# Two halves of a product added by ScalarE and VectorE, not by a matrix product, in the small expert blocks of a mixture-of-experts layer

## The chip, the cores and the metric

The kernel runs on one core of a Trainium2 chip. The metric is the device time of one launch in microseconds (us); the time given for a kernel is the median of its runs. Beside the plain runs, one execution was profiled: the profile shows for each engine when it worked and what it waited for. The engines are TensorE (PE, with its weight loads as PEld), VectorE (DVE), ScalarE (ACT), GpSimd (POOL), and SyncE (SP), which here only issues transfers.

## The reference

One layer of a diffusion backbone over 1024 tokens of width 1024, in fp32: a modulated RMSNorm, one input projection, two kinds of mixing (differential attention and retention), an output projection with a gated residual, and then a mixture of experts. Only the last part matters here. Each token picks 8 of 64 experts; every expert is a small gated network of inner width 256, and a shared one is applied to all tokens:

```python
xb = h_pad[tok]
yb = (jax.nn.silu(xb @ w1[e]) * (xb @ w3[e])) @ w2[e]
acc.at[tok].add(yb * wt[:, None])
```

The result is added to the residual and normalised once more.

## The kernel before, in words

**Precision.** PE multiplies in a reduced fp32 format. So each operand is split in two: hi is the operand as ACT copies it into that format, lo is what DVE finds as the difference. A product of x and w is then hi x hi + hi x lo + lo x hi. The weights of an expert (3 MB, loaded as `eraw`) are split in six pieces of 128x1024 each, ACT's copy on L1110 and DVE's subtraction on L1111; both write tiles named `w`. While the blocks of one expert run, the pieces of the next are split between them.

**Blocks.** The experts are ranked by their number of tokens and each rank has a fixed capacity, 384 down to 32 rows, cut in blocks of 128 rows and a rest. A list puts large and small experts in turn. After the shared expert's 8 blocks come 96 blocks of routed rows; 33 of these have a rest of 64 or 32 rows and run as `n == 64`.

**A step of the loop** (L1181 and around) does for block i: the up product (`up()`: 8 slices of the width, w1 and w3 side by side in a PSUM bank of 128x512), the gate (`gate()`: SiLU on ACT, L1207, product on DVE, L1209, into `hn`), the transposes of `hn` on PE (L1165) with their split on ACT and DVE (L1169, L1170, `ehT`), and, one step later, the down product (`down()`: two banks `py` of 128x512). DVE scales each bank by the routing weight and the layer's gate into `y` (L1232), and POOL adds the rows of `y` to the token table `acc` in DRAM (the scatter, L1120). The rows of the block after next are gathered on POOL (L1149, `xg`) and transposed on PE (`tr`, L1165, then `xT`). A scatter starts when all scatters of the expert before have landed. There are two `y` buffers, used in turn, so a block's `y` can be written when the scatter of the block two before it has landed.

**Blocks of 64.** Here hi and lo of x stand side by side as 128 columns of one operand. Two products per slice of the width, with the hi and lo of w, then give x_hi w in rows 0 to 63 of the bank and x_lo w in rows 64 to 127, and the two halves of rows have to be added. Before, ACT copies rows 64 to 127 of the bank into a buffer `fb` (L1185), and PE multiplies it with a matrix `fold` (L1190) that moves row 64 + r onto row r and adds it in the bank. This is done once for `up` and twice for `down`, 99 times in all. The zeros in the rest of `fb` and of `fold` keep the other rows as they are; in the gate all 128 rows are worked on.

**Order.** The order of the instructions on each engine is set by a scheduler that simulates them when the program is built; it is fixed then, and each engine works through its own list in turn. So an instruction that waits also holds up what stands behind it on its engine.

Of the kernel before, what the change touches and what calls it, by code (L numbers as in the profile page):

```python
# [9 lines left out]
F32 = mybir.dt.float32  # L10
F32R = mybir.dt.float32r
# [3 lines left out]
AF = mybir.ActivationFunctionType  # L15
OP = mybir.AluOpType
# [4 lines left out]
P = 128  # L21
# [63 lines left out]
def hybrid_layer_kernel(ctx: ExitStack, tc: tile.TileContext, A, out, dbg=None):  # L85
    nc = tc.nc
    pe, dve, act, pool, sp = nc.tensor, nc.vector, nc.scalar, nc.gpsimd, nc.sync
# [19 lines left out]
    def open_pool(ctx, name, side=None, space=None):  # L107

        kw = {k: v for k, v in (("side", side), ("space", space)) if v is not None}
        return ctx.enter_context(tc.tile_pool(name=name, bufs=1, reuse_waits="tile", **kw))  # L110
# [17 lines left out]
    consts = ctx.enter_context(tc.tile_pool(name="consts", bufs=1, side="left"))  # L128
# [4 lines left out]
    def C(k):  # L133
        o, n = CST_OFF[k]
        return cst[:, o:o + n]

    ident = C("ident")
# [70 lines left out]
    def project(t, w, n0=0, n1=512):  # L208
        his, los = w
        hh, hl = hT(t)  # L210
        ps = psa.tile([P, 512], F32, name="pp", tag="pp", bufs=2)
        for k in range(KT):
            wh, wl = his[k // 2][:, k % 2, n0:n1], los[k // 2][:, k % 2, n0:n1]
            pe.matmul(ps[:, n0:n1], hh[:, k, :], wh, start=(k == 0), stop=False)  # L214
            pe.matmul(ps[:, n0:n1], hh[:, k, :], wl, start=False, stop=False)  # L215
            pe.matmul(ps[:, n0:n1], hl[:, k, :], wh, start=False, stop=(k == KT - 1))  # L216
        return ps
# [50 lines left out]
    for kind in range(2):  # L268
        for fb in range(2):
            dve.tensor_scalar(Wd[:, kind, :, fb], lg[:, 4 * fb:4 * fb + 4], pw[:, 2 * kind + fb:2 * kind + fb + 1],  # L270
                              None, op0=OP.mult)
# [158 lines left out]
    for i, g in enumerate(pairs):  # L430
        for t in (2 * g - 2, 2 * g - 1):
            if t < 0:
                ps = project(t, W, 256, 512)
# [31 lines left out]
    for i in range(0, TAB_ROWS // P, 126):  # L465
        n = min(126, TAB_ROWS // P - i)
# [21 lines left out]
    for t in range(-2, NT):  # L488
        ada_rest(VADA)
        ps = project(t, W)  # L490
# [13 lines left out]
        for h in range(H):  # L504
            pe.matmul(pk[:, h, :], kd[:, h].rearrange("p a b -> p (a b)"), v[:, h * P:(h + 1) * P],
                      start=True, stop=True)
# [24 lines left out]
    for t in reversed(range(NT)):  # L531
# [4 lines left out]
        ps = project(t, W)  # L536
# [69 lines left out]
    for t in range(-2, NT):  # L606
        ps = project(t, W)
# [6 lines left out]
        c = slice((t + 2) * P, (t + 3) * P)  # L614
# [16 lines left out]
    def row_tile(pl, i, name, **kw):  # L631
        t = pl.tile([P, D], F32, name=name, **kw)
        sp.dma_start(t, bass.AP(tensor=rows_d.tensor, offset=rows_d.offset + i * D, ap=[[0, P], [1, D]]))
        return t
# [167 lines left out]
    def bank(ring, shape):  # L802
        n = ring_at[ring] = ring_at.get(ring, -1) + 1
        b = RINGS[ring][n % len(RINGS[ring])]
        return (psd if b < 6 else ps8).tile(shape, F32, name=ring, tag=f"bank{b}")
# [51 lines left out]
    pm = open_pool(m_ctx, "pm", "right")  # L857
    pl_ = open_pool(m_ctx, "pl", "right")
    pc = open_pool(c_ctx, "pc", "right")
    y2 = Ring(pm, "y0", "y1")  # L860
    g2r = row_tile(pm, 3, "g2r")
# [189 lines left out]

    tokc = consts.tile([P, NT], I32, name="tokc")
    dve.tensor_copy(tokc, C("tok"))

    fold = consts.tile([P, P], F32R, name="fold")
    dve.tensor_scalar(fold, ident, 0.0, None, op0=OP.mult)
    dve.tensor_copy(fold[64:128, 0:64], ident[64:128, 64:128])

    hT4 = Ring(pm, "g0", "g1", "g2", "g3")

    fbs, fb_n = [], [0]

    def fold_buffer():
        if not fbs:
            for tag in ("so", "mks"):
                fbs.append(pl_.tile([P, 512], F32R, name="fb", tag=tag))
                dve.tensor_scalar(fbs[-1][0:64], g2r[0:64, 0:512], 0.0, None, op0=OP.mult)
        fb_n[0] += 1
        return fbs[fb_n[0] % 2]

# [46 lines left out]
    def scatter_add(y, idx, j=None):  # L1117


        x = pool.indirect_dma_start(out=acc, out_offset=bass.IndirectOffsetOnAxis(ap=idx, axis=0), in_=y,  # L1120
                                    in_offset=None, compute_op=OP.add)
        if j is None:
            return
        mine = added.setdefault(j, [])
        for o in mine:
            tc.declare_no_dep(x.ins, o.ins, reason="the blocks of an expert have no row in common")
        for o in added[j - 1] if j else x1_stores:
            tc.add_manual_dep(x.ins, o.ins.name, mybir.DependencyInfo(
                mybir.DependencyClass.Sync, mybir.DependencyReason.DATA), reason="rows of the expert before")
        mine.append(x)  # L1130

    class Block:
# [40 lines left out]
        def product(self, ps, ops, whi, wlo, nk):  # L1173
            if self.n > 64:
                seq = [(o, w) for o, w in ((0, whi), (0, wlo), (1, whi))]
            else:
                seq = [(0, whi), (0, wlo)]
            po = ps[:ops[0].shape[2]]
            for k in range(nk):
                for j, (o, w) in enumerate(seq):  # L1180
                    pe.matmul(po, ops[o][:, k, :], w(k), start=(k == 0 and j == 0),  # L1181
                              stop=(k == nk - 1 and j == len(seq) - 1))
            if self.n == 64:
                fb = fold_buffer()
                act.activation(fb[64:128], ps[64:128], AF.Copy)  # L1185
                self.fb = fb

        def fold(self, ps):
            if self.n == 64:
                pe.matmul(ps, fold, self.fb, start=False, stop=True, skip_group_check=True)  # L1190

        def tr(self):
            if self.xT is None:
# [7 lines left out]

        def gate(self):
            pu = self.pu
            self.fold(pu)
            sl = pm.tile([P, 256], F32, name="sl", tag="sl", bufs=2)
            m = P if self.n == 64 else self.n
            act.activation(sl[:m], pu[:m, 0:256], AF.Silu)  # L1207
            self.hn = pm.tile([P, 2, P], F32, name="hn", tag="hn", bufs=2)
            dve.tensor_tensor(self.hn[:m].rearrange("p k q -> p q k"),  # L1209
                              pu[:m, 256:512].rearrange("p (q k) -> p q k", k=2),  # L1210
                              sl[:m].rearrange("p (q k) -> p q k", k=2), op=OP.mult)
# [4 lines left out]
        def down(self):  # L1216
            n = self.n
            hi2, lo2 = self.W[2:]
            y = y2.tile([P, D], F32, name="y")
            ps, fbs = [], []  # L1220
            for i in range(2):
                c = slice(i * 512, (i + 1) * 512)
                py = bank("py", [P, 512])
                self.product(py, self.hT, lambda k: hi2[k][:, c], lambda k: lo2[k][:, c], 2)
                ps.append(py)
                fbs.append(getattr(self, "fb", None))
            for i in range(2):
                self.fb = fbs[i]
                self.fold(ps[i])
                c = slice(i * 512, (i + 1) * 512)  # L1230
                if YMODE[i]:
                    dve.scalar_tensor_tensor(y[:n, c], ps[i][:n], self.wt, g2r[:n, c], op0=OP.mult, op1=OP.mult)  # L1232
                else:
                    act.activation(y[:n, c], ps[i][:n], AF.Copy, scale=self.wt)
                    pool.tensor_tensor(y[:n, c], y[:n, c], g2r[:n, c], op=OP.mult)
            scatter_add(y[:self.rows], self.idx[:self.rows], self.j)
# [198 lines left out]
    with tc.For_i(0, n_over, 1) as j:  # L1435
# [15 lines left out]
        for q in range(2):  # L1451
            pt = bank("tr", [P, 4, P])
            for i in range(4):
                k = 4 * q + i
                pe.transpose(pt[:, i, :], xg[:, k * P:(k + 1) * P], ident)
            act.activation(xT[:, 4 * q:4 * q + 4, :], pt, AF.Copy)
        pu = bank("up", [P, 512])
        for i in range(2):
            for k in range(KT):
                pe.matmul(pu[:, i * 256:(i + 1) * 256], xT[:, k, :], w13[:, i, k, :], start=(k == 0),  # L1460
                          stop=(k == KT - 1))
        s_ = pf.tile([P, 256], F32, name="fs")
        act.activation(s_, pu[:, 0:256], AF.Silu)
        hn = pf.tile([P, 2, P], F32, name="fhn")
# [7 lines left out]
        y = pf.tile([P, D], F32, name="fy")  # L1472
        for n in range(2):
            c = slice(n * 512, (n + 1) * 512)
# [52 lines left out]
```

## Time and profile before

| | us |
|---|---|
| median of 3 runs (lowest to highest) | 1809.39 (1807.29 to 1812.17) |
| the profiled execution | 1804.75 |
| its span, from first to last instruction | 1802.9 |
| routed experts, in the profile | from about 914 to 1775 |
| PE, DVE, ACT busy over the span | 1667.1, 1349.9, 960.8 |

The busy share of PE is that of pipelined products: one takes some 0.4 us from start to end, and the next starts while it runs. Where a row gives several numbers behind a window they are the busy time of each engine in it; a window without the shares is read against its own length. The chain of waits is followed back from the last instruction, at each step to what released it.

### The profile page before, as it was taken

Reading aid. Unit: us, or ns where it says so; the run is one execution under the profiler, and the core shown is the slowest. Engines: PE = TensorE matmul, PEld = TensorE weight load, DVE = VectorE, ACT = ScalarE, POOL = GpSimd, SP = SyncE. Lnnn points to the kernel's source line nnn. Section 1 sums busy time; section 2 is a strip of 40 time slices with the busy share of each in tenths; the row PEclk is TensorE's granted clock in tenths of the full one; section 3 lists DMA queues with packets and bytes.
Section 4 is the critical chain, followed back from the end, with each engine's and each line's share of the span. In section 5 each row is a group of like instructions: output and inputs, shape, how many; then the busy total and the mean of one; then the engine's idle time right before and its main releaser. Section 6 shows DMA issues by size and latency. Waiting matters only on the chain.

```text
span 1802.9 us, 23066 instructions
## 1 busy us (share of the span) xinstructions
PE 1667.1 (92%) x8022; PEld 1267.4 (70%) x8022; DVE 1349.9 (75%) x2080; ACT 960.8 (53%) x1537; POOL 535.6 (30%) x384
## 2 busy tenths in 40 slices
PE   5899889999799989999899999999999999999992
PEld 3687667788466658777677767777777777777771
DVE  7876666650887866987478888888888988878873
ACT  6532233321688752233266686677675666566652
POOL 0100113300221230457235334333445343332331
PEclk9999999999899999999899999999999999999996
DMA  9665545800111144334889999999999999999976
GB/s 311 211 213 179 182 148 116 181 24 27 69 53 59 36 166 163 105 122 115 268 234 310 317 327 329 319 316 295 342 318 329 356 330 326 329 303 320 315 213 213
DMA packets 128413, 400.57 MB, mean 222 GB/s; under 512 B 13110, under 2 KB 49654, under 8 KB 103336
## 3 DMA queue, kind: packets, MB, share of 16 engines
q1 hardware_dynamic: 81000, 297.10, 46.0%
q0 software_dynamic: 46144, 97.80, 23.2%
q10 hardware_dynamic: 1152, 4.19, 0.6%
q8 instruction: 64, 1.05, 0.2%
q14 instruction: 53, 0.43, 0.1%
HBM read 324.45 MB, written 74.60 MB: 221 GB/s over the span
## 4 chain that ended last, share of the span: by engine, by line
PE 54%; DMA 16%; DVE 14%; ACT 7%; issue 5%; POOL 3%; SPq 1%; POOLq 0%; DVEq 0%; ACTq 0%
PE up L1181 18%; DMA acc<-y,sidx 9%; PE py L1181 8%; PE pp L215 4%; PE pp L214 3%; PE pp L216 3%; PE tr L1165 3%; DVE w L1111 3%; PE pS L97 3%; PE py L97 3%; DMA eraw<-in_exp_w_dram 2%; PE pu L97 2%; ACT w L1110 2%; DVE nmx L697 2%; PE ptt L97 1%
## 5 line engine op out<-in xcount | busy, mean ns | idle before, releaser
L1181 PE MATMUL up<-w,xT 128*128 128x512 f32 (+1 forms) x2136 | 531.1, 398 | 7.7 <-DVE xT L1170 7.3
L1111 DVE TENSOR_TENSOR w<-eraw,w 128x1024 fp32r<-128x1024 f32 x390 | 459.7, 1216 | 42.8 <-ACT w L1110 42.2
L1110 ACT ACTIVATE w<-eraw 128x1024 fp32r<-128x1024 f32 x390 | 400.1, 1056 | 118.4 <-PE up L1181 60.6
L1181 PEld LDWEIGHTS up<-w,xT 128*128 128x128 f32 (+1 forms) x2136 | 381.4, 183 | 106.3 <-DVE xT L1170 12.9
L1120 POOL DMA_INDIRECT acc<-y,sidx x96 | 205.3, 2138 | 484.0 <-DMA acc<-y,sidx 198.7
L1181 PE MATMUL py<-w,ehT 128*128 128x512 f32 (+1 forms) x1116 | 296.0, 408 | 0.8 <-DVE ehT L1170 0.8
L1181 PEld LDWEIGHTS py<-w,ehT 128*128 128x128 f32 (+1 forms) x1116 | 200.4, 187 | 48.5 <-DVE ehT L1170 1.1
L1232 DVE SCALAR_TENSOR_TENSOR y<-py,swt,g2r 128x512 f32<-128x512 f32 (+2 forms) x192 | 137.6, 739 | 62.6 <-DMA acc<-y,sidx 46.6
L214 PE MATMUL pp<-whi,hTh 128*128 128x512 f32 (+1 forms) x448 | 178.9, 400 | 1.3 <-ACT hTh L371 1.2
L216 PE MATMUL pp<-whi,hTl 128*128 128x512 f32 (+1 forms) x448 | 177.0, 397 | 1.2 <-DVE hTl L372 1.2
L215 PE MATMUL pp<-wlo,hTh 128*128 128x512 f32 (+1 forms) x448 | 177.8, 398 | 0.0
L697 DVE TENSOR_REDUCE nmx<-pS 128x1 f32<-128x1280 f32 x64 | 95.1, 1486 | 74.6 <-PE pS L97 74.4
L1149 POOL DMA_INDIRECT xg<-h2tab,sidx x96 | 128.4, 1338 | 72.6 <-PE tr L1165 48.1
L1170 DVE TENSOR_TENSOR xT<-tr,xT 128x512 fp32r<-128x512 f32 (+1 forms) x167 | 104.2, 654 | 17.7 <-ACT xT L1169 17.4
L1207 ACT ACTIVATE sl<-up 128x256 f32<-128x256 f32 (+1 forms) x104 | 39.7, 382 | 139.6 <-PE up L1181 138.8
L159 POOL TENSOR_TENSOR rs_r<-rs_v,mhalf 128x1 f32<-128x1 f32 (+1 forms) x34 | 28.2, 830 | 276.0 <-DVE rs_v L157 160.5
L969 POOL DMA_INDIRECT slots<-dat,ad x64 | 72.0, 1126 | 97.4 <-DVE dat L966 55.2
L216 PEld LDWEIGHTS pp<-whi,hTl 128*128 128x128 f32 x448 | 84.3, 188 | 23.6 <-issue 2.6
L214 PEld LDWEIGHTS pp<-whi,hTh 128*128 128x128 f32 x448 | 84.4, 189 | 22.8 <-issue 2.6
L97 PE MATMUL pS<-K,qsl 128*128 128x512 f32 x336 | 93.1, 413 | 7.3 <-ACT an L704 4.8
L1165 PEld LDWEIGHTS tr<-cst,xg 128*128 128x128 f32 (+2 forms) x800 | 79.7, 140 | 28.2 <-issue 7.1
L215 PEld LDWEIGHTS pp<-wlo,hTh 128*128 128x128 f32 x448 | 84.9, 190 | 19.5 <-issue 2.0
(308 smaller groups left out, 2327.6 us busy)
## 6 DMA issues: line engine op xcount, KB each, us to landing
eraw<-in_exp_w_dram SPq DMA_DIRECT2D x192, 1024.0 KB, 11.0
ada_l<-in_ada_w_dram SPq DMA_DIRECT2D x64, 256.0 KB, 3.0
wraw<-in_w_in_dram SPq DMA_DIRECT2D x24, 512.0 KB, 3.9
aw<-in_ada_w_dram SPq DMA_DIRECT2D x8, 1024.0 KB
qsp<-qs POOLq DMA_DIRECT2D x32, 256.0 KB, 4.0
qsl<-qsp POOLq DMA_DIRECT2D x7, 1024.0 KB, 5.3
xt<-in_x_dram SPq DMA_DIRECT2D x8, 512.0 KB, 10.0
wor<-in_w_out_dram SPq DMA_DIRECT2D x8, 512.0 KB, 3.2
```

Source lines behind the costliest of these rows:

```text
L97: i = getattr(self.eng, name)(*args, **kw)
L214: pe.matmul(ps[:, n0:n1], hh[:, k, :], wh, start=(k == 0), stop=False)
L215: pe.matmul(ps[:, n0:n1], hh[:, k, :], wl, start=False, stop=False)
L216: pe.matmul(ps[:, n0:n1], hl[:, k, :], wh, start=False, stop=(k == KT - 1))
L697: dve.tensor_reduce(self.nmx, self.pS, axis=AX.X, op=OP.max, negate=True)
L1110: act.activation(hi, raw, AF.Copy)
L1111: dve.tensor_sub(lo, raw, hi.bitcast(F32))
L1120: x = pool.indirect_dma_start(out=acc, out_offset=bass.IndirectOffsetOnAxis(ap=idx, axis=0), in_=y, in_offset=None, compute_op=OP.add)
L1149: self.load = pool.indirect_dma_start(out=self.xg[:self.n], out_offset=None, in_=h2tab, in_offset=bass.IndirectOffsetOnAxis(ap=self.idx, a ...
L1165: pe.transpose(pt[:, i, :], src[:rows, k * P:(k + 1) * P], ident[:rows, :rows])
L1181: pe.matmul(po, ops[o][:, k, :], w(k), start=(k == 0 and j == 0), stop=(k == nk - 1 and j == len(seq) - 1))
L1232: dve.scalar_tensor_tensor(y[:n, c], ps[i][:n], self.wt, g2r[:n, c], op0=OP.mult, op1=OP.mult)
```

## The change

In a block of 64 ACT copies rows 64 to 127 of the bank straight to where the sum is to stand, rows 0 to 63 of a buffer in SBUF, and DVE adds rows 0 to 63 of the bank to them in place. For `up` that buffer is `fb`, of which the gate's product then overwrites the first 256 columns and serves as `hn`; the zeros now fill its rows 64 to 127, for the transposes. For `down` the buffer is `y` itself, which DVE then scales in place. The matrix `fold` and its products are gone, and the gate works on 64 rows.

```diff
-    fold = consts.tile([P, P], F32R, name="fold")
-    dve.tensor_scalar(fold, ident, 0.0, None, op0=OP.mult)
-    dve.tensor_copy(fold[64:128, 0:64], ident[64:128, 64:128])
...
-                fbs.append(pl_.tile([P, 512], F32R, name="fb", tag=tag))
-                dve.tensor_scalar(fbs[-1][0:64], g2r[0:64, 0:512], 0.0, None, op0=OP.mult)
+                fbs.append(pl_.tile([P, 512], F32, name="fb", tag=tag))
+                dve.tensor_scalar(fbs[-1][64:128], g2r[64:128, 0:512], 0.0, None, op0=OP.mult)
...
-            if self.n == 64:
-                fb = fold_buffer()
-                act.activation(fb[64:128], ps[64:128], AF.Copy)
-                self.fb = fb
-
-        def fold(self, ps):
-            if self.n == 64:
-                pe.matmul(ps, fold, self.fb, start=False, stop=True, skip_group_check=True)
+
+        def fold(self, ps, to):
+            act.activation(to, ps[64:128], AF.Copy)
+            dve.tensor_tensor(to, ps[0:64], to, op=OP.add)
...
         def gate(self):
             pu = self.pu
-            self.fold(pu)
             sl = pm.tile([P, 256], F32, name="sl", tag="sl", bufs=2)
-            m = P if self.n == 64 else self.n
+            if self.n == 64:
+                hn = fold_buffer()
+                self.fold(pu, hn[0:64])
+                pu = hn[0:64]
+                self.hn = hn[:, 0:256].rearrange("p (k q) -> p k q", k=2)
+            else:
+                self.hn = pm.tile([P, 2, P], F32, name="hn", tag="hn", bufs=2)
+            m = self.n
             act.activation(sl[:m], pu[:m, 0:256], AF.Silu)
-            self.hn = pm.tile([P, 2, P], F32, name="hn", tag="hn", bufs=2)
...
             for i in range(2):
-                self.fb = fbs[i]
-                self.fold(ps[i])
                 c = slice(i * 512, (i + 1) * 512)
+                if n == 64:
+                    self.fold(ps[i], y[0:64, c])
+                    ps[i] = y[:, c]
```

The scheduler also sets the instructions in another order. The first place is DVE's list where two experts with one block of 64 each follow a large one (`w` is a piece of a weight split, `xT` and `ehT` the split of transposed operands; in the new kernel lines are up to five lower). Before:

```order
L1170 TENSOR_TENSOR xT_9845<-tr,xT_9845 128x8x64
L1209 TENSOR_TENSOR hn<-up,sl 128x128x2
L1232 SCALAR_TENSOR_TENSOR y<-py,swt,g2r 64x512
L1111 TENSOR_TENSOR w_9808<-eraw_9589,w_9806 128x1024
L1232 SCALAR_TENSOR_TENSOR y<-py,swt,g2r 64x512
L1170 TENSOR_TENSOR ehT_9888<-tr,ehT_9888 128x2x64
L1111 TENSOR_TENSOR w_9809<-eraw_9589,w_9807 128x1024
```

And now, for the same block:

```order
L1165 TENSOR_TENSOR xT_9827<-tr,xT_9827 128x8x64
L1181 TENSOR_TENSOR fb<-up,fb 64x512
L1181 TENSOR_TENSOR y<-py,y 64x512 x2
L1205 TENSOR_TENSOR fb<-fb,sl 64x128x2
L1228 SCALAR_TENSOR_TENSOR y<-y,swt,g2r 64x512 x2
L1106 TENSOR_TENSOR w_9791<-eraw_9573,w_9789 128x1024
L1165 TENSOR_TENSOR ehT_9870<-tr,ehT_9870 128x2x64
L1106 TENSOR_TENSOR w_9792<-eraw_9573,w_9790 128x1024
```

Three additions have come in between the operand split and the next operand copy, and the piece of the weight split that stood between the two scalings now stands behind both.

The second place is ACT's list late in the stage, where an expert of 128 + 64 rows and one of 128 take turns; it is the block of 64. Before:

```order
L1169 ACTIVATE xT_15416<-tr 128x512 x2
L1185 ACTIVATE fb<-py 64x512
L1110 ACTIVATE w_15369<-eraw_15220 128x1024
L1185 ACTIVATE fb<-py 64x512
L1169 ACTIVATE ehT_15462<-tr 128x256
L1110 ACTIVATE w_15369<-eraw_15220 128x1024
```

And now:

```order
L1164 ACTIVATE xT_15383<-tr 128x512 x2
L1180 ACTIVATE y<-py 64x512
L1105 ACTIVATE w_15336<-eraw_15188 128x1024
L1180 ACTIVATE y<-py 64x512
L1164 ACTIVATE ehT_15429<-tr 128x256
L1105 ACTIVATE w_15336<-eraw_15188 128x1024
```

The places are the same; the two copies write `y` where they wrote `fb`, and the same weight piece and operand copy stand behind them.

More of the change, by code (lines that the diff above doesn't have):

```diff
@@ L1219, in down @@
             y = y2.tile([P, D], F32, name="y")
-            ps, fbs = [], []
+            ps = []
             for i in range(2):
@@ L1225, in down @@
                 ps.append(py)
-                fbs.append(getattr(self, "fb", None))
             for i in range(2):
-                self.fb = fbs[i]
-                self.fold(ps[i])
                 c = slice(i * 512, (i + 1) * 512)
+                if n == 64:
+                    self.fold(ps[i], y[0:64, c])
+                    ps[i] = y[:, c]
                 if YMODE[i]:
```

## The prediction

> **What bounds the kernel now.** I read the page's shares first, then the expert stage in windows of 100 us, because the change touches only that stage.
>
> ```profile
> PE 1667.1 (92%) x8022; PEld 1267.4 (70%) x8022; DVE 1349.9 (75%) x2080; ACT 960.8 (53%) x1537; POOL 535.6 (30%) x384
> ...
> 900.00:1000.00 100.00, 97.57 (x475) 74.83 (x474) 79.01 (x101) 65.21 (x95) 41.93 (x22) 1.00 0.91 277
> 1000.00:1100.00 100.00, 97.03 (x470) 73.28 (x467) 87.71 (x109) 72.24 (x105) 40.28 (x24) 1.00 0.99 322
> 1100.00:1200.00 100.00, 99.17 (x479) 76.27 (x477) 85.19 (x109) 73.84 (x109) 37.89 (x23) 1.00 0.98 312
> 1200.00:1300.00 100.00, 99.52 (x483) 75.92 (x482) 86.96 (x112) 69.74 (x103) 39.93 (x24) 1.00 0.98 325
> 1400.00:1500.00 100.00, 99.84 (x498) 75.87 (x497) 88.66 (x112) 62.13 (x89) 40.80 (x22) 1.00 1.03 344
> 1600.00:1700.00 100.00, 96.40 (x454) 73.69 (x452) 82.01 (x103) 64.05 (x91) 33.49 (x22) 1.00 0.97 317
> ```
>
> The columns after the window's length are busy us of PE, PEld, DVE, ACT and POOL, then granted clock, DMA share and GB/s. Over the whole span DVE is at 75%, but in this stage it is at 85 to 89%, close behind PE. The DMA moves 344 GB/s in one window and 312 to 325 in the windows with many folds, so it is not what holds those back.
>
> Where do the folds lie? The same windows, for the folding products alone (PE busy us and count, then PEld):
>
> ```profile
> 900.00:1000.00 100.00, 6.27 (x13) 2.42 (x13) 1.00 0.91 277
> 1000.00:1100.00 100.00, 9.19 (x20) 3.73 (x20) 1.00 0.99 322
> 1100.00:1200.00 100.00, 10.29 (x22) 4.17 (x22) 1.00 0.98 312
> 1200.00:1300.00 100.00, 7.91 (x17) 3.18 (x17) 1.00 0.98 325
> 1600.00:1700.00 100.00, 5.50 (x11) 2.05 (x11) 1.00 0.97 317
> ```
>
> 59 of the 99 folds stand in the 300 us from 1000 to 1300; I call that the dense part. There the work repeats with a period of 42.2 us: an expert with rows for 128, 128 and 64, then two experts with one block of 64 each. The first row below is the large expert of one period, the second the pair of small ones, and the third is a stretch of the same work without folds:
>
> ```profile
> 1151.40:1177.30 25.90, 25.87 (x127) 20.42 (x127) 21.03 (x28) 15.71 (x23) 8.66 (x6) 1.00 0.98 325
> 1177.30:1193.60 16.30, 16.09 (x78) 11.92 (x78) 14.67 (x19) 14.43 (x22) 7.00 (x4) 1.00 0.96 290
> ...
> 1390.85:1428.09 37.24, 37.24 (x186) 28.81 (x185) 34.39 (x44) 24.59 (x35) 10.47 (x7) 1.00 1.02 344
> ```
>
> In the pair DVE is busy 14.67 of 16.30 us (90%) and ACT 14.43 (89%): a small expert brings as many weights to split as a large one, and one block of work to hide that behind. So PE's 99% there is a long queue of overlapping products, while the chain of waits shows who sets the pace (start, us, what):
>
> ```profile
> 1174.08 1.36 PE py L1181 x5
> 1175.44 0.23 PE up L1190
> ...
> 1187.86 1.90 ACT w L1110 x2
> ...
> 1192.24 0.60 ACT fb L1185
> ...
> 1192.88 0.50 PE py L1190
> ```
>
> In the large expert the chain is PE; in the pair it runs through ACT's weight splits and copies, and the fold starts only when ACT's copy is done. [...]
>
> **The change part by part.** These groups carry the prices (count, busy us, mean ns of one):
>
> ```profile
> L1190 PE MATMUL py<-fb,fold 128*128 128x512 f32 x66 | 31.8, 482 | 5.1 <-ACT fb L1185 3.6
> L1190 PE MATMUL up<-fb,fold 128*128 128x512 f32 x33 | 15.2, 460 | 3.6 <-ACT fb L1185 3.1
> L1185 ACT ACTIVATE fb<-py 64x512 fp32r<-64x512 f32 x66 | 38.3, 591 | 6.3 <-PE py L1181 5.1
> L1232 DVE SCALAR_TENSOR_TENSOR y<-py,swt,g2r 64x512 f32<-64x512 f32 x66 | 47.7, 734 | 22.3 <-DMA acc<-y,sidx 16.3 <-PE py L1190 6.0
> ...
> L1170 DVE TENSOR_TENSOR xT<-tr,xT 128x512 fp32r<-128x512 f32 x131 | 86.0, 683 | 16.4 <-ACT xT L1169 16.2
> L231 DVE TENSOR_TENSOR ro<-ro,rt 128x512 f32<-128x512 f32 x24 | 16.6, 690 | 0.6
> ```
>
> *Removed from PE:* 66 + 33 = 99 folding products. One with its operand ready takes 0.23 us of PE's time (the row at 1175.44), the 480 ns being latency that overlaps its neighbours. That is 99 x 0.23 = 22.8 us, 13.6 of them in the dense part, plus the 3.6 + 3.1 us that PE idles for the copy. Two small DVE instructions at the very start vanish too, at no worth here.
>
> *Kept on ACT:* 99 copies of 64x512 at 0.59 us; only where they write changes (the buffer for the hidden layer, or y), so ACT's load stays. Their place moves, which matters below.
>
> *Added to DVE:* 99 additions of 64x512. No addition from PSUM onto SBUF stands in the trace; the nearest are the subtraction that reads PSUM (683 ns) and the addition in SBUF (690 ns), both 512 wide. As busy time, where neighbours overlap, the first costs 86.0 / 131 = 0.656 us and the second 16.6 / 24 = 0.69. I take 0.65; bounds are 0.60 (nearly back to back) and 0.69. Total 99 x 0.65 = 64 us on DVE, against 22.8 us off PE. The scaling by the routing weight (L1232) and the gate's product now read SBUF instead of PSUM; by 683 against 690 ns that is no gain.
>
> [...]
>
> *The sum for the dense part.* DVE is busy there 87.71 + 85.19 + 86.96 = 259.9 of 300 us. With 59 x 0.65 = 38.4 it needs 298.2 (295.3 to 300.6 by the bounds). It cannot be full, because it waits for others:
>
> ```profile
> DVE w L1111 <- ACT w L1110: 17.1, 16, 2.5
> DVE hn L1209 <- ACT sl L1207: 13.5, 16, 2.0
> DVE xT L1170 <- ACT xT L1169: 8.9, 14, 2.4
> ...
> 1050.00:1100.00 50.00, 48.90 (x232) 37.04 (x231) 45.97 (x57) 37.43 (x55) 17.40 (x12) 1.00 1.01 334
> ```
>
> These are DVE's three longest waits from 950 to 1300, all for ACT (total us, times, longest), and the fullest 50 us that it shows in the stage: 45.97, 92%. Some of the waits shrink when DVE runs late, since ACT is then ahead; but the gate now goes copy (ACT), addition (DVE), SiLU (ACT), product (DVE), so ACT also waits for DVE, where that turn was PE's. The share that DVE can reach lies between 92% and 100%. I take the middle, 96%: 298.2 / 0.96 = 310.6, so the dense part grows by 10.6 us. Bounds: 298.2 / 0.92 = 324.1, +24.1 us; at 100% it is -1.8 (and -4.7 with the cheap addition). PE's 13.6 us saved there are hidden under DVE, so they earn nothing.
>
> *Elsewhere.* 13 folds lie in 900 to 1000, where DVE rises from 79.0 to 87.5 and stays below 92%, so PE's saving can show: 13 x 0.23 = 3.0 us at most, of which I take 2 (bounds 0 and 3). From 1500 on the end is set by scatters that follow each other:
>
> ```profile
> 1588.53 12.36 DMA acc<-y,sidx
> ...
> 1601.65 10.26 DMA acc<-y,sidx
> ...
> 1617.20 11.50 DMA acc<-y,sidx
> ...
> 1629.46 10.80 DMA acc<-y,sidx
> ...
> 1607.73 0.59 ACT L1185 ACTIVATE fb<-py 64x512 fp32r<-64x512 f32 x1
> 1609.44 0.59 ACT L1185 ACTIVATE fb<-py 64x512 fp32r<-64x512 f32 x1
> 1612.03 0.74 DVE L1232 SCALAR_TENSOR_TENSOR y<-py,swt,g2r 64x512 f32<-64x512 f32 x1 [2.55 <-DMA acc<-y,sidx]
> ```
>
> The first rows are the chain, the last three the block of 64 in it. Two y buffers exist; this block's y is free when the scatter of 1601.65 has landed, at 1611.91. Before, ACT's copies went to a buffer of their own and ran at 1607.73; now they write y, so the first waits until 1611.91, and behind it on ACT stand a weight split, the second copy and the next operand copy (the second excerpt of the order). Copy 0.59, split 1.06, copy 0.59 lead to 1614.2; addition and two scalings, 0.65 + 2 x 0.66, to 1616.2. The scatter went at 1617.20, so 1 us is to spare and the chain holds: 0. If that cover were gone, each of the few blocks of 64 there would pay what is late, about 1 us. At the very end an addition (0.65) takes the place of a fold (0.48): +0.3 for the two halves.
>
> Together: 10.6 - 2 + 0.3 = +8.9, or 9 us on the profiled execution of 1804.75 (span 1802.9), that is 1813.8. The median of the runs is 1809.39, 4.6 above that execution; with the same 9 us I predict **1818.4 us**.
>
> **The rivals.**
>
> *PE is the bound and its relief shows.* For it: PE at 97 to 99.5% in the dense part, and folds on the chain. Against: DVE's need of 295.3 to 298.2 us leaves only 2 to 5 us of those 300, even if it never waits. With the 3 us of the first window: -5 to -8, about 1803. Chance 0.13.
>
> *Nothing to see.* DVE gets through at 98 or 99%, since the new order takes PE's waits for copies away; 298.2 / 0.985 = 302.7, less 2: about +1, 1810. Chance 0.22.
>
> *ACT is held by the y buffers.* Each of the 66 copies now waits for a scatter that landed late, with weight splits queued behind it and PE waiting for those. In the scatter-bound part this hold is 4.2 us (1607.73 to 1611.91) and ACT has idle time for it (64 of 100 us busy); it decides only if it also falls into the pairs, where ACT is at 89%. For it: ACT is on the chain there. Against: in the dense part DVE's y hardly waits for a scatter now. With DVE at the lower share, 92%, that is +22 to +30: 1832 to 1840. Chance 0.15.
>
> **How the numbers follow.** The forecast, a DVE-bound dense part, has 0.50 and its own range is 1813 to 1829 (+4 to +20). Beyond 0.3% (5.4 us) a change can be told from none. Slower: 0.45 of the forecast and the 0.15 of the held ACT, 0.60. Same: the 0.22 and 0.05 of the forecast, 0.27. Faster: 0.13. The range that should hold 8 in 10 goes from 1803, most of the relief case included, to 1836, into the held-ACT case.
>
> **What would show it.** Right: L1190 is gone; a new group of 99 additions of about 690 ns on DVE; DVE at 94 to 98% between 1000 and 1300 and on the chain there; the period of 42.2 us grown to 43 or 44; the pair of small experts grown from 16.3 us while the large expert's 25.9 stay; the scatter chain after 1515 as before at about 28.6 us for three blocks. Wrong: the period shrinks towards 40 (relief), or DVE stays near 88% while the time grows and ACT's y copies wait for scatters (the third rival), or the additions cost much less than 0.60 us.

## The result, and the profile after

The changed kernel takes 1836.69 us (median of 5 runs, 1832.03 to 1841.58); the kernel before, run beside it, 1810.63 us (1807.29 to 1812.17). The ratio is 1.0141, with a 95% interval of 1.0120 to 1.0162: 26 us slower. The forecast was 9 us slower, within 1803 to 1836. The direction was right, the size nearly three times too small, and the time stands 0.7 us outside the range.

To see where the time went I cut the routed experts at the starts of four scatters (numbered from 0, the shared expert's eight among them). POOL's rows of before and of after (start, us, engine, line; in brackets the idle time ahead and what ended it):

```profile
934.50 2.32 POOL L1120 DMA_INDIRECT acc<-y,sidx  x1 [2.91 <-DVE y L1232]
1380.63 1.79 POOL L1120 DMA_INDIRECT acc<-y,sidx  x1 [3.83 <-DVE hn L1209]
1573.06 1.57 POOL L1120 DMA_INDIRECT acc<-y,sidx  x1 [11.30 <-DMA acc<-y,sidx]
1771.73 1.33 POOL L1120 DMA_INDIRECT acc<-y,sidx  x1 [2.83 <-DVE y L1232]
```

```profile
946.07 4.22 POOL L1115 DMA_INDIRECT acc<-y,sidx  x1 [3.06 <-DVE y L1228]
1427.60 1.57 POOL L1115 DMA_INDIRECT acc<-y,sidx  x1 [7.00 <-DMA acc<-y,sidx]
1623.47 1.56 POOL L1115 DMA_INDIRECT acc<-y,sidx  x1 [11.75 <-DMA acc<-y,sidx]
1809.05 1.33 POOL L1115 DMA_INDIRECT acc<-y,sidx  x1 [3.37 <-DVEq L1431]
```

These are blocks 10, 60, 80 and 103. From block 10 to 60 I say *dense* (25 of the 33 blocks of 64, 75 of the 99 additions; it holds the 300 us of the forecast), from 80 to 103 *tail* (the other 8). Both kernels were profiled twice:

| us | before | before again | after | after again |
|---|---|---|---|---|
| start of the first scatter | 827.7 | 835.0 | 842.9 | 837.7 |
| first scatter to block 10 | 106.9 | 104.9 | 103.1 | 106.4 |
| dense, 10 to 60 | 446.1 | 447.2 | 481.5 | 478.0 |
| 60 to 80 | 192.4 | 190.2 | 195.9 | 193.6 |
| tail, 80 to 103 | 198.7 | 199.7 | 185.6 | 189.7 |
| from there to the end | 31.2 | 31.1 | 30.7 | 30.4 |

By the means the dense part costs +33.1 us, the tail gives 11.6 back, 60 to 80 costs 3.5. The start lies ahead of every changed product. Two executions of one program differ there by 7.3 us (before) and 5.2 (after), and over all eighteen profiles told of here it lay between 819 and 848 us, once at 823 us with the new products (e10). So I leave it out of every comparison below; that none of the 9 us between the means belongs to the change is not shown.

The engines after, first over the span, then in windows (busy us of PE, PEld, DVE, ACT, POOL; granted clock, DMA share, GB/s):

```profile
PE 1661.4 (90%) x7923; PEld 1261.0 (69%) x7923; DVE 1407.7 (77%) x2177; ACT 953.1 (52%) x1537; POOL 571.8 (31%) x384
...
1000.00:1100.00 100.00, 87.40 (x401) 64.12 (x400) 90.75 (x121) 68.19 (x101) 44.49 (x21) 0.97 0.95 310
1100.00:1200.00 100.00, 88.50 (x424) 66.79 (x423) 87.96 (x117) 60.16 (x91) 45.17 (x22) 1.00 0.88 267
1200.00:1300.00 100.00, 88.88 (x417) 67.79 (x416) 87.12 (x114) 63.76 (x94) 39.45 (x22) 0.97 0.90 282
```

DVE has more to do and yet is hardly fuller (87 to 91%, from 85 to 88%), PE fell from 97 to 99.5% to 87 to 89%, ACT and the DMA fell too. Over 100 us nobody is full, so everybody waits for somebody. The groups of the new work after:

```profile
L1181 DVE TENSOR_TENSOR y<-py,y 64x512 f32<-64x512 f32 x66 | 43.3, 676 | 9.9 <-ACT y L1180 9.8
L1181 DVE TENSOR_TENSOR fb<-up,fb 64x512 f32<-64x512 f32 x33 | 22.3, 676 | 3.4 <-ACT fb L1180 3.4
L1228 DVE SCALAR_TENSOR_TENSOR y<-y,swt,g2r 64x512 f32<-64x512 f32 x66 | 46.4, 735 | 0.1
L1180 ACT ACTIVATE y<-py 64x512 f32<-64x512 f32 x66 | 38.1, 587 | 15.5 <-PE py L1176 8.2 <-DMA acc<-y,sidx 3.9 <-issue 3.3
```

99 additions, 65.6 us busy, 0.66 each. The prices were right. The waits from 1000 to 1300 (total us, times, longest), first before, then after:

```profile
ACT w L1110 <- DMA eraw<-in_exp_w_dram: 4.4, 3, 2.1
PE up L1181 <- DVE w L1111: 0.3, 1, 0.3
```

```profile
ACT w L1105 <- DMA eraw<-in_exp_w_dram: 24.1, 10, 4.4
DVE xT L1165 <- ACT xT L1164: 13.8, 12, 3.4
DVE ehT L1165 <- ACT ehT L1164: 9.3, 7, 3.8
PE up L1176 <- DVE w L1106: 10.9, 7, 1.6
PE up L1176 <- DVE xT L1165: 9.3, 9, 2.0
```

New is above all that ACT waits for weights: 24.1 us instead of 4.4 (23.5 in the second profile of the change). One such hold in the timeline of after, DVE and SP first, then ACT, then who follows:

```profile
1197.43 1.22 DVE L1106 TENSOR_TENSOR w<-eraw,w 128x1024 fp32r<-128x1024 f32 x1
1198.67 2.55 SPq L1076 DMA_DIRECT2D eraw<-in_exp_w_dram  x2
...
1211.74 2.01 ACT L1105 ACTIVATE w<-eraw 128x1024 fp32r<-128x1024 f32 x2 [2.68 <-DMA eraw<-in_exp_w_dram]
1213.66 0.58 ACT L1164 ACTIVATE xT<-tr 128x512 fp32r<-128x512 f32 x1
...
1214.27 0.69 DVE L1165 TENSOR_TENSOR xT<-tr,xT 128x512 fp32r<-128x512 f32 x1 [2.61 <-ACT xT L1164]
...
1215.01 2.80 PE L1176 MATMUL up<-w,xT 128*128 128x512 f32 x11 [1.97 <-DVE xT L1165]
```

DVE ends a weight split at 1198.65, which frees a raw tile (a buffer for loaded weights); SP, which waits for such splits (263 us of the 300 from 1000 to 1300, 249 before the change), issues the next loads at 1198.67; ACT waits for a load until 1211.74, with the operand copy of the next block queued behind; DVE idles for that copy, and PE for DVE. That gave the first theory of the mechanism, a loop: DVE late, loads late, ACT held, DVE idle and later still.

### The profile page after: what moved, and what is told of

The parts are those of the page before. It is cut to its first block, busy times and chain, and to the rows that moved or that the text cites. A ratio compares the mean times of both kernels' runs of the same rounds, so it can differ in the third digit from the quotient of the medians.

```text
span 1839.7 us, 22811 instructions
## 1 busy us (share of the span) xinstructions
PE 1661.4 (90%) x7923; PEld 1261.0 (69%) x7923; DVE 1407.7 (77%) x2177; ACT 953.1 (52%) x1537; POOL 571.8 (31%) x384
## 3 DMA queue, kind: packets, MB, share of 16 engines
q8 instruction: 63, 1.03, 0.2%
## 5 line engine op out<-in xcount | busy, mean ns | idle before, releaser
L1176 PE MATMUL up<-w,xT 128*128 128x512 f32 (+1 forms) x2136 | 540.0, 403 | 30.7 <-DVE w L1106 14.6
L1176 PEld LDWEIGHTS up<-w,xT 128*128 128x128 f32 (+1 forms) x2136 | 383.7, 185 | 136.7 <-DVE xT L1165 24.5
L1115 POOL DMA_INDIRECT acc<-y,sidx x96 | 225.5, 2349 | 451.9 <-DMA acc<-y,sidx 118.4
L1176 PE MATMUL py<-w,ehT 128*128 128x512 f32 (+1 forms) x1116 | 289.4, 406 | 7.9 <-DVE ehT L1165 7.5
L1144 POOL DMA_INDIRECT xg<-h2tab,sidx x96 | 146.4, 1525 | 88.8 <-PE tr L1160 66.5
L1228 DVE SCALAR_TENSOR_TENSOR y<-py,swt,g2r 128x512 f32<-128x512 f32 (+1 forms) x126 | 90.3, 738 | 35.4 <-DMA acc<-y,sidx 28.9
L1160 PE MATMUL tr<-cst,xg 128*128 128x128 f32 (+2 forms) x800 | 93.6, 255 | 7.3 <-DVE xT L1165 4.8
L1204 ACT ACTIVATE sl<-up 128x256 f32<-128x256 f32 (+1 forms) x71 | 27.1, 381 | 139.9 <-PE up L1176 130.1
```

The costliest lines, as they stand in the source:

```text
L1144: self.load = pool.indirect_dma_start(out=self.xg[:self.n], out_offset=None, in_=h2tab, in_offset=bass.IndirectOffsetOnAxis(ap=self.idx, a ...
L1160: pe.transpose(pt[:, i, :], src[:rows, k * P:(k + 1) * P], ident[:rows, :rows])
```

## The experiments

Most of the kernels below have one profile, so a difference between two stretches has to be read against what equal work differs by: 1.1 and 3.5 us in the table above, but 9.5 us in one case (e2 below, whose dense part is the old way). I trust differences well over 10 us. The forecast for dense was +8.6 us (10.6 less 2). The kernel before took 1820.2 us beside e1 to e3 and 1824.4 beside e5 to e8, where it took 1810.6 beside the change, so the times expected are to be read by the ratio.

**Which part of the kernel pays: e1 and e2.** The new way only for the experts ahead of place 40 in the order (all of dense, none of the tail), and only for those behind. A before-again, e4, shows what repeats.

```diff
+    LATE = 40
...
+        def new(self, what):
+            return self.n == 64 and (self.j < LATE)
...
-            if self.n == 64:
+            if self.n == 64 and not self.new(what):
                 fb = fold_buffer()
```

> The new way of adding the halves only in the blocks of 64 of the first 39 experts (the dense part, up to about 1380 us of the profile before), the fold on PE in the last blocks of 64. Theory A (the dense part costs some 35 us, and the 13 us that the late part of the changed kernel gives back come from the new way in the late blocks themselves): about 1810.6 + 35 = 1846. Theory B (the late part runs faster only because the dense part before it ran late): about 1836, as with the full change. Theory C (the dense part costs less than it seems, and the 11 us by which the two profiles differ before the first routed expert belong to the change): 1815 to 1825.

> The new way only in the eight blocks of 64 of the last 25 experts, the fold on PE in the dense part. Theory A (the late gain is the new way's own): 1810.6 - 13 = about 1798. Theory B (the late gain is an echo of the late dense part): 1810, no change. If the adds cost there too, 1813 or more.

> The kernel before once more, for a second profile. If the 11 us by which the first scatters of the changed kernel's profile are late (before any changed instruction has run) are chance, this profile's stage of routed experts starts anywhere between that of the two (first scatter 828 to 843 us); if it starts at 828 again, the change moves the part ahead of it too.

e1: ratio 1.0167 (1.0110 to 1.0224); dense 475.7, tail 200.8. e2: ratio 0.9895 (0.9839 to 0.9951), median 1801.32 us; dense 456.2, tail 186.7. e4: dense 447.2, tail 199.7. So the dense blocks pay and the late blocks gain by themselves, each without the other. That rests on the stretches: e1's interval alone also holds theory B's time (1836, a ratio of 1.014). e2, the new way in the eight late blocks only, is faster than the kernel before, by 19 us beside it, of which its shorter tail explains 12.5.

**By how many additions: e3.** The up product keeps its fold on PE, only `down` is new.

```diff
+        def new(self, what):
+            return self.n == 64 and (what == "down")
```

> Both banks of the down product are added by ACT and DVE, the up product keeps its fold on PE: 66 of the 99 additions, but no turn of ACT, DVE, ACT, DVE in the gate. Theory L (DVE's load is the price, in proportion): two thirds of the dense cost, about 1810.6 + 23 - 10 = 1824. Theory G (the hand-overs of the gate are the price): under 1816. Theory Y (ACT's copies into y wait for scatters): about as the full change, 1833 or more.

e3: ratio 1.0074 (1.0046 to 1.0102), about 14 us, which is theory L's size (its 1834.8 us is Y's number only because the kernel before was slower, too); dense 470.7 (+24 for 50 additions, against +33 for 75), tail 192.0 (7 of the 11.6 us gained). The price goes about with the count: 0.48 and 0.44 us for an addition of 0.66. So it is not the gate's longer chain alone (copy, addition, SiLU, product), which this kernel doesn't have.

**Load or hand-over: e5 and e6.** e5 is the change with its additions left out (so hi rows are missing in blocks of 64). e6 is the kernel before with its folds, and idle additions beside them.

```diff
         def fold(self, ps, to):
             act.activation(to, ps[64:128], AF.Copy)
-            dve.tensor_tensor(to, ps[0:64], to, op=OP.add)
```

```diff
+                for h in (0, 256):
+                    dve.tensor_tensor(self.hn[0:64].rearrange("p k q -> p (k q)"), pu[0:64, h:h + 256],
+                                      g2r[0:64, h:h + 256], op=OP.add)
...
+                if n == 64:
+                    dve.tensor_tensor(y[0:64, c], ps[i][0:64], g2r[0:64, c], op=OP.add)
```

> The changed kernel with its 99 VectorE additions left out: ScalarE's copies still write y and the hidden layer's buffer, and everything behind them stands as in the change, but the hi rows are never added (so the outputs of blocks of 64 lack them). Dense below means from the scatter of block 10 to that of block 60 in the trace: 446 us before, 481.5 after. Theory L (VectorE's load is the price): dense falls to 446 or less, since PE is also relieved of its folds, and with the gain of the late blocks the time is 1785 to 1803. Theory H (the new hand-over is the price: copies into y and the hidden buffer that both engines share, and ScalarE's list): dense stays at 465 or more, time 1820 or more.

> The kernel before, folding products and all, with idle additions put on VectorE at the places of the new ones: 66 of 64x512 into y ahead of the scaling (which overwrites them), and two of 64x256 for each of the 33 blocks into the gate's buffer. Theory L: dense 470 to 490 us, time 1832 to 1850, no gain in the late blocks. Theory H: dense 446 to 455, time 1808 to 1818.

e5: ratio 0.9906 (0.9875 to 0.9936), dense 444.6, tail 188.9. e6: ratio 1.0268 (1.0229 to 1.0307), dense 497.3, tail 197.0. Take DVE's additions away, and dense is back at the value of before; put idle ones on the old kernel, and dense grows by 51 us. So DVE's load sets the price as far as these two tell. And as in the change, DVE with more to do is not fuller. Windows of e5 and of e6 (columns as above):

```profile
1100.00:1200.00 100.00, 94.21 (x454) 73.17 (x453) 84.70 (x108) 69.95 (x106) 49.30 (x25) 0.98 1.00 320
```

```profile
1100.00:1200.00 100.00, 89.10 (x416) 67.25 (x415) 84.39 (x118) 61.33 (x89) 33.44 (x21) 0.98 0.89 270
```

84% DVE in both, though e6 asks more of it. It came out 7 us above theory L's upper end in dense, and in time 9 us by the ratio (1.0268 of 1810.6 is 1859): e6 has the load without PE's relief. Its load isn't quite that of the change either: the two additions in the gate take 0.82 us instead of 0.66, and ACT's SiLU waited for them, 8.4 us in six waits in dense.

One thing moves with every edit: the scheduler sets the lists anew. I compared DVE's lists from block 10 to 60, by what each instruction writes and with the additions left out. The longest common order holds 85 of 100 instructions for e5 and the change, 81 for e6 and the kernel before, and 84 for the two kernels themselves. So e5 and e6 alone can't tell the load from the order that came with it. The pairs e7 and e8 and e13 and e14 below can be read without this doubt: each keeps 99 of 100 instructions of DVE, and 96 or 97 of ACT, in the order of its original.

**What the folds cost PE: e11.** The kernel before with the folding products left out and nothing in their place (the lo rows are missing in blocks of 64).

```diff
         def fold(self, ps):
             if self.n == 64:
-                pe.matmul(ps, fold, self.fb, start=False, stop=True, skip_group_check=True)
+                pass
```

> The kernel before with its 99 folding products left out, and nothing put in their place: ScalarE's copies still go to their own buffer, and the lo rows of the blocks of 64 are not added (so their outputs lack them). For the late blocks, called tail: from the scatter of block 80 to that of block 103, 198.7 us before, 185.6 after, 188.9 with the change but without its additions. Theory P (the folding product, and what waits for it, is what the late blocks gain): tail 191 or less. Theory Q (it is the copy that writes y directly and the order on VectorE and GpSimd that follows): tail 196 to 201. Dense: 440 to 446 by both, since VectorE's load there is unchanged.

e11: dense 432.2, tail 198.6; one run at 1779.68 us beside one at 1805.49. Both theories had dense unchanged, and both were wrong there: the folds, with what waits for them, cost 14 us of it, so PE's relief is real. The tail stays, so the late gain does not come from PE (theory Q). Of these 14 us the change keeps little: with the new copies and without additions (e5) dense is 444.6. In e5 ACT's copies into y wait for scatters, 15.5 us in 1000 to 1300:

```profile
ACT y L1180 <- DMA acc<-y,sidx: 15.5, 7, 2.9
```

**Does the transfers' time multiply the price: e7 to e10.** w2 is not loaded, its splits read w1's raw tile (so the kernel leaves out w2): a third less weight traffic, in the kernel before (e7) and the changed one (e8). e9 and e10 are the same pair with four raw tiles in turn, so that two experts are held as in the original and not three.

```diff
-        raw = hv_tile([P, 2, D], "eraw2")
-        sp.dma_start(raw, w2.rearrange("(p k) d -> p k d", p=P))
-        return raws + [raw]
+        return raws + [raws[0].rearrange("p (a k) f -> p a (k f)", a=2)]
```

```diff
-        return hv.tile(shape, F32, name=name, tag=f"hv{(slot[0] - 1) % 6}")
+        return hv.tile(shape, F32, name=name, tag=f"hv{2 + (slot[0] - 3) % 4}")
```

> The kernel before with a third of the experts' weight traffic left out: w2 is not loaded, its splits read w1's raw tile (so the experts' outputs use wrong numbers). This is the base for the next run; the DMA was at 312 to 344 GB/s in the dense part and PE at 99%, so all theories expect dense 430 to 446 us and a time of 1790 to 1810.

> The changed kernel with the same third of weight traffic left out. Theory W (a loop: VectorE late, so raw weight buffers come free late, weights land late, ScalarE waits for them at the head of its list, VectorE and PE idle behind it): with transfers a third shorter the loop has slack, and dense is at most 15 us over the run with the same third left out, the time at most 5 over it (less where the late blocks gain). Theory L without that loop: dense is still 30 to 36 us over it, the time 20 to 27 over it.

> The kernel before with a third of the weight traffic left out as before (w2 not loaded), and now only four raw weight tiles in turn instead of six, so that, as in the original, the weights of two experts are held and not of three. Base for the next run; all theories expect dense 440 to 452 us.

> The changed kernel with the same two edits. With six tiles and less traffic the additions cost 7 us of dense (450.3 against 443.4). Theory T (the amplifier is the transfers' time: a third less of it leaves slack): dense at most 12 us over the run with four tiles before it. Theory D (it is the depth, the third expert's raw tiles held ahead): dense 20 us or more over it.

e7: 1805.09 us, dense 443.4. e8: 1798.57 us, dense 450.3. With a third of the traffic gone the same additions in nearly the same order cost 7 us of dense, and the changed kernel is no longer slower; so the order, without the full traffic, is not the price. e9: dense 453.3; e10: 462.7, so +9.4 with four tiles, below the 12 of theory T: it is not the depth. The windows of e8:

```profile
1000.00:1100.00 100.00, 88.80 (x420) 66.38 (x419) 93.91 (x124) 68.43 (x102) 48.56 (x21) 0.98 0.73 228
1100.00:1200.00 100.00, 94.89 (x463) 73.15 (x462) 95.35 (x127) 68.57 (x103) 56.89 (x25) 1.00 0.81 237
1200.00:1300.00 100.00, 94.15 (x463) 72.28 (x462) 95.73 (x130) 73.03 (x111) 52.19 (x24) 1.00 0.80 236
```

DVE is at 94 to 96%, the share that the forecast took, and the price is the forecast's, as far as one profile tells. What the forecast missed needs the full transfers (e13 and e14 put them back).

**Is it the loop through the raw tiles: e13 and e14.** The traffic is whole again: w2 is copied by the same queue to a spare place in memory. But this third waits for no split, and six raw tiles hold three experts.

```diff
+    spare = [dram.tile([256, D], F32, name=f"spare{i}") for i in range(8)]
...
-        raw = hv_tile([P, 2, D], "eraw2")
-        sp.dma_start(raw, w2.rearrange("(p k) d -> p k d", p=P))
-        return raws + [raw]
+        spare_n[0] += 1
+        sp.dma_start(spare[spare_n[0] % 8], w2)
+        return raws + [raws[0].rearrange("p (a k) f -> p a (k f)", a=2)]
```

> The kernel before with w2's splits reading w1's raw tile, and w2 itself copied to a spare place in memory by the same queue (it goes to no raw tile and waits for no split, so that six raw tiles hold three experts): the traffic is whole again. Base for the next run: dense 440 to 455 us by both theories, DMA share 0.95 or more.

> The changed kernel with the same edits. Theory G (the price is multiplied because late splits hold loads back): dense at most 15 us over the run before it, VectorE at 92% or more from 1000 to 1300. Theory C (the full traffic is enough): dense 25 us or more over it, VectorE at 87 to 90%.

e13: dense 454.3, DMA share 0.93 to 0.95. e14: dense 479.9, so +25.6, DVE 88 to 91%. The price is back, as theory C had it, although ACT hardly waits for weights. My loop theory (G) falls as the whole account. Another wait of ACT stands in its place (one of e14's windows, its waits, then its timeline):

```profile
1100.00:1200.00 100.00, 91.14 (x446) 69.78 (x445) 91.46 (x121) 67.13 (x100) 53.81 (x24) 1.00 0.89 288
```

```profile
ACT w L1107 <- DMA eraw<-in_exp_w_dram: 0.9, 1, 0.9
```

```profile
1063.59 0.60 ACT L1182 ACTIVATE y<-py 64x512 f32<-64x512 f32 x1 [3.22 <-DMA acc<-y,sidx]
...
1158.40 0.59 ACT L1182 ACTIVATE y<-py 64x512 f32<-64x512 f32 x1 [3.87 <-issue]
...
1207.05 0.59 ACT L1182 ACTIVATE y<-py 64x512 f32<-64x512 f32 x1 [6.08 <-issue]
```

Three copies into y are held for 13.2 us together. The first is put down to a scatter. For the other two the profile names no releaser, but for the second its times do: the scatter of the block two before, issued at 1144.97, took 13.4 us to land, until 1158.3. The third I read the same way, since y's tile is the one thing that this copy needs beside a product.

**Is it that hold: e15 and e16.** As e13 and e14, with four raw tiles, and the freed space used for two more y tiles.

```diff
+            y_n[0] += 1
+            y = (hv.tile([P, D], F32, name="y", tag=f"hv{y_n[0] // 2 % 2}") if y_n[0] % 2 and self.j
+                 else y2.tile([P, D], F32, name="y"))
```

> The kernel before with w2 copied to a spare place (as before, its splits read w1's raw tile), the raw tiles of w1 and w3 reduced to four, and the two tiles that this frees used as two more y tiles. Base for the next run: dense 440 to 455 us by both theories.

> The changed kernel with the same edits. Theory H: no copy into y waits over 1 us for a scatter, dense 6 to 15 us over the run before it (if weights come late with four raw tiles, those waits show in its place and dense lies between). Theory C: dense 22 us or more over it, without holds of ScalarE over 2 us.

e15: dense 463.7, above the 440 to 455 that both theories had. e16: dense 464.1, so +0.4, with the traffic whole (DMA share 0.88 to 0.96). No copy into y waits for a scatter any more, and DVE is at 92 to 95% (e16's windows, then its waits):

```profile
1100.00:1200.00 100.00, 94.00 (x458) 72.10 (x457) 94.53 (x125) 65.27 (x98) 52.78 (x24) 1.00 0.92 298
1200.00:1300.00 100.00, 93.25 (x456) 71.17 (x455) 92.67 (x125) 68.46 (x105) 53.34 (x24) 1.00 0.96 308
```

```profile
ACT w L1108 <- DMA eraw<-in_exp_w_dram: 24.5, 16, 2.6
```

That is theory H as to y, with a limit: +0.4 is below its 6 to 15. ACT waits for weights for 24.5 us here, as long as in the change (the longest 2.6 us, there 4.4), and yet the additions cost nothing: the kernel that they are compared with, e15, waits for weights too (14.7 us) and has already paid (463.7 against 446). The sum of that wait over 300 us is therefore no measure of the price.

**Once more the change: e12.**

> The changed kernel once more, for what two profiles of one program differ by. If the parts are properties of the program: dense 476 to 487 us (481.5 in the first), tail 182 to 190 (185.6). If the stage's start (842.9 in the first, ahead of every changed instruction) belongs to the execution and not to the change, it may lie anywhere from 819 to 848; if to the change, at 840 to 848.

e12: dense 478.0, tail 189.7, start 837.7: the parts repeat, the start does not. Ratio 1.0113 (1.0005 to 1.0220, two runs).

## Why the prediction was right or wrong

*Bound and direction: right.* DVE's load sets the price in the dense part: without the additions (e5) it is gone, with two thirds of them (e3) it is 24 of 33 us, with idle ones (e6) it comes without the change. By its occupancy DVE (85 to 88%) stood behind PE (97 to 99.5%) from 1000 to 1300 before the change, and yet the work added to it cost 33 us, while the folds on PE cost 14 (e11).

*Prices of the operations: right.* Additions 0.66 us each as busy time, taken 0.65 (0.60 to 0.69); copies unchanged at 0.59. The trace before did hold an addition from PSUM onto SBUF, which the prediction overlooked: 16 of 128x512 on L1313, 687 ns each, within its bounds. The scaling of a block of 64 takes 735 ns from SBUF and took 734 from PSUM, so moving its source saved nothing, as the sum had it.

*The step that failed: the share that DVE can reach.* The forecast divided DVE's need by 96%, midway between its fullest 50 us before (92%) and 100%, and did so for the 300 us as a whole. In the change DVE reached 87 to 91%, below both ends. The runs show what the step left out: in e8, with the DMA share at 0.73 to 0.81, DVE reached 94 to 96%, and the additions cost 7 us. With the full traffic they cost 33 us in the change (DMA share 0.88 to 0.95) and 26 in e14 (0.88 to 0.89). I had set the DMA aside because it moved 312 to 325 GB/s here and 344 elsewhere; its share in the same rows, 0.98 to 0.99 (1.03 in 1400 to 1500), I did not weigh. The sum had no term for ACT's waits on loads (24.1 us in the change) and on scatters (13.2 us in e14, read as above).

*Where the price lies: forecast right by the division below, size wrong.* The prediction had the pair of small experts grow and the large expert stay. Divided at the first up product of a block on PE (in after, where a large expert's first runs alone, at its second), three periods (blocks 32 to 46) took, in us (the prediction's 25.9 and 16.3 were cut at other instructions):

| | large expert | pair | ACT's waits for weights in the pair | holds of copies into y in the pair |
|---|---|---|---|---|
| before | 27.5, 27.2, 27.2 | 15.0, 15.0, 15.0 | none | none |
| after | 26.8, 26.8, 26.9 | 20.4, 20.2, 20.2 | 4.5, 4.2, 4.4 | none |
| after again | 26.9, 26.8, 27.5 | 20.3, 19.8, 20.5 | 4.4, 3.9, 4.6 | none |
| e8, less traffic | 25.9, 25.8, 25.9 | 16.7, 16.7, 16.7 | none | none |
| e14, spare copy | 25.9, 25.8, 26.9 | 20.7, 23.1, 16.7 | none | 3.9, 6.1, 0.3 |

By this division all the growth is in the pair; divided at the lone product of 1172.28, the pair of after takes 13.7 us and the large expert behind it 33.5 (DVE 73% and 92%), so the growth lies around that hand-over. Before, DVE was busy for 83% of the large expert's time and 89% of the pair's; after, for 95% and 76%. So in the large expert DVE did reach the forecast's share. In the pair it idles, while the DMA share stands at 0.99 and 1.01 there (0.83 to 0.88 in the large expert). The additions by themselves lengthen the pair by 1.7 us (e8; it was 15.0 in e7, too), and the rest of the 5.3 comes with ACT's late weights. In e14 the pair is longer than 16.7 us by about as much as the copies into y are held (4.0 for 3.9, 6.4 for 6.1, none for 0.3). The period grew not to 43 or 44 us but to 47 (scatters of the same place in the order after: 1153.28, 1200.12 and 1247.19). PE's waits in one pair of after, before a product of its second expert and at its end, before the second product of the next large expert (the first ran alone at 1172.28):

```profile
1167.43 2.82 PE L1176 MATMUL up<-w,xT 128*128 128x512 f32 x11 [1.62 <-DVE xT L1165]
...
1178.99 3.72 PE L1176 MATMUL up<-w,xT 128*128 128x512 f32 x15 [1.61 <-DVE w L1106]
```

*PE's relief: wrong in size.* I put it at nothing in the dense part, hidden under DVE. e11 shows that the folds cost 14 us there, about the 13.6 us of PE time that the forecast had counted (for 59 of the 75 folds) and set aside. The change gives that back: by the new copies (e5 is 12 us over e11) and by the additions (35 us over e5).

*ACT held by the y buffers (third rival): not what the change pays, but a mechanism.* In the change copies into y waited for scatters for 3.9 us in all, and for 3.3 more in one wait without a named releaser; in the pairs above not at all. The time of 1836.7 fell into this rival's 1832 to 1840 by another way: that was luck. In e5 and e14 the hold is there, 15.5 and, read as above, 13.2 us.

*The tail: wrong.* Taken as 0, it gains 11.6 us. With six raw tiles each run with the new way there gained: 185.6 to 192.4, where the old way takes 197.0 to 206.8. With four raw tiles (e10, 199.8; e16, 204.4) there is no gain over e9 (199.0) and e15 (204.0). The rows of POOL for one block of 64 and its neighbours, before and after:

```profile
1612.64 2.52 POOL L1120 DMA_INDIRECT acc<-y,sidx  x1 [8.04 <-DMA acc<-y,sidx]
1615.47 1.43 POOL L1149 DMA_INDIRECT xg<-h2tab,sidx  x1 [0.30 <-issue]
1617.20 1.46 POOL L1120 DMA_INDIRECT acc<-y,sidx  x1 [0.30 <-DVE w L1111]
...
1629.46 1.57 POOL L1120 DMA_INDIRECT acc<-y,sidx  x1 [9.55 <-DVE hn L1209]
```

```profile
1659.13 1.58 POOL L1115 DMA_INDIRECT acc<-y,sidx  x1 [8.16 <-DVE w L1106]
1661.02 0.99 POOL L1144 DMA_INDIRECT xg<-h2tab,sidx  x1 [0.30 <-issue]
1662.83 2.53 POOL L1115 DMA_INDIRECT acc<-y,sidx  x1 [0.82 <-DVE y L1228]
...
1672.71 1.59 POOL L1115 DMA_INDIRECT acc<-y,sidx  x1 [6.09 <-DMA acc<-y,sidx]
```

The second scatter goes 3.70 us after the first instead of 4.56, and the next 9.9 us later instead of 12.3. It is not PE's fold (e11) and not the additions (e5 gains too), so by exclusion it hangs on the copy that writes y and the order that follows. Why the next scatter can go sooner stays open.

*What stays open in the dense part.* Shown: the additions are needed (e3, e5), and so are the full transfers (e8 against e14, with the order kept). Not shown by a run of its own: that in the change itself the late weights carry the rest. The pairs above say so, but no run took the waits away at full traffic with all else unchanged. Nor was the order of the change tried at full traffic without the additions: e5 has an order of its own. Nor is it shown that y alone carried the price in e14: e16 has two more y tiles, but also four raw tiles, and the kernel that it is compared with had grown to 463.7 by then. The granted clock was 0.97 to 1.00 in the windows of the change (0.93 to 0.98 in its second profile), from 1.00 before; e5 had 0.98 in the window above and paid nothing.

## What to carry to other kernels

When an engine that is busy for 85 to 88%, as DVE here, is given more work, do the sum for each part of the repeating stretch, not for the mean: here, divided as above, the large expert took its additions without growing (27.3 to 26.8 us), and the pair paid for all (15.0 to 20.3). Work out what the engine can reach from everything that it exchanges tiles with, not from its own fullest window (92% here, where the change reached 87 to 91%), and read the DMA share beside the GB/s: here, with 0.98 to 0.99 and 312 to 325 GB/s before the change, the added time came out nearly four times over the sum (33 us for 8.6), and with 0.73 to 0.81 and 228 to 237 GB/s (e8) within it (7 us). Such a trade (one engine's load for another's) need not be made everywhere: here the same edit cost 33 us where DVE is loaded and brought 12 where the scatters set the pace, so doing it only there (e2) beats the kernel before by about 1% (0.9839 to 0.9951 of its time).

## What the runs showed of the hardware

In the change an addition of 64x512 from PSUM onto SBUF took 676 ns on DVE, and 0.66 us of its time where neighbours overlapped; in e6 one of 64x256 took 408 ns. SiLU of 64x256 from SBUF took 411 ns on ACT, and of 128x256 from PSUM 384 (both in after).

The issue of a scatter on POOL took 1.5 to 1.6 us in some places and 2.5 or more in others. In the rows above, those of 2.5 us (1612.64 and 1662.83) ran for most of their time while DVE split weights from SBUF to SBUF, and that of 1659.13 while it read PSUM. The rows of DVE (before, then after):

```profile
1613.68 3.48 DVE L1111 TENSOR_TENSOR w<-eraw,w 128x1024 fp32r<-128x1024 f32 x3
```

```profile
1659.85 1.38 DVE L1181 TENSOR_TENSOR y<-py,y 64x512 f32<-64x512 f32 x2
...
1662.82 2.35 DVE L1106 TENSOR_TENSOR w<-eraw,w 128x1024 fp32r<-128x1024 f32 x2
```

It is not a rule: the scatter of 1672.71 took 1.59 us although DVE split weights from 1669.36 to 1673.98. Over the routed scatters of both profiles, all 100 above 2 us overlapped a split for at least 0.3 of their time, but so did many short ones, ten of them for over 0.7. That the one causes the other was not tried.
